# Moving the stationary operands of 256-column matmuls by 29 elements in SBUF

## The chip, the cores and the metric

The kernel runs on one core of one Trainium2 chip. The metric is device time in microseconds for one execution, as the median of several runs. A profile is one execution recorded by the hardware profiler; its span runs from the first to the last instruction and is a little shorter than the time of that execution.

## The reference, cut to what matters

The kernel computes two layers of a small encoder for 512 tokens of 1024 features, in float32. Each layer is a token mixer followed by a SwiGLU feed-forward, and each of the four parts has a norm with scale and shift ahead of it and a norm with a gate behind it.

```
def swiglu(h, w_gate, w_up, w_down):
    return (jax.nn.silu(h @ w_gate) * (h @ w_up)) @ w_down

for i in range(DEPTH):
    h = rms_norm(x, mix_pre_g[i]) * (1.0 + scale) + shift
    y = stick_breaking_mixer(...) if i % 2 == 0 else token_mixing_mixer(...)
    x = x + gate * rms_norm(y, mix_post_g[i])
    h = rms_norm(x, ffn_pre_g[i]) * (1.0 + scale) + shift
    y = swiglu(h, w_gate[i], w_up[i], w_down[i])
    x = x + gate * rms_norm(y, ffn_post_g[i])
```

The token mixer of layer 1 computes u and v as gelu(h @ w_in), mixes v over positions, and multiplies the two. The feed-forward is 2816 wide: gate and up are products of 512 x 1024 with 1024 x 2816 each, so they hold much of the arithmetic.

## The kernel before

Every float32 matrix product is made of three matmuls in the reduced fp32r format. An operand is split into a high part (a copy rounded to fp32r, made by ScalarE) and a low part (the difference, made by VectorE). `mm3` then adds high by high, low by high and high by low into one PSUM bank. In the profile these matmuls have one line, L107, and they are told apart by tiles: `r<-Sh,wh` writes bank `r`, streams `Sh` and holds `wh` as its stationary operand. TensorE first loads a stationary operand of 128 x 128 (the engine name PEld in the profile) and then streams the other operand past it, 256 or 512 columns at a time.

Weights arrive by DMA in `raw` buffers (`wload`, `block_loads`), in the order of a list named `stream`. `wemit` takes the next raw buffer, asks `wtile` for a pair of buffers `wh` and `wl`, and lets ScalarE and VectorE fill them. A pair rotates through five buffers (later six) of 1088 elements per partition. Only 1024 are needed for a weight tile, so a tile may begin a little way into its buffer, and `wtile` has an argument `at` for that.

In the kernel before, the start depends on how the tile is used:

- Weights of 512-column matmuls (q and k, v, the output projection, both down projections where they are not made by blocks) begin at element 16 of their buffers.
- Weights of 256-column matmuls begin at element 0. These are the gate and up weights of the first three units of each feed-forward (key `wgu`, tile `gu` in PSUM), the weights of u (key `win_u`, tile `u`), and the blocks of all later gate and up units (tile `r`).

The later gate and up units are made by `seven`. It takes a gate tile and an up tile together, as a two-by-two block product, and makes it with seven block products instead of eight. `blocks` prepares the weights for one such unit: `x` holds two blocks as they came, `b21` holds one more in a buffer of its own with 512 elements, and `t13` and `t24` hold sums of blocks. All of them are split into high and low parts. Each product runs over four slices of 128, three matmuls each, so a unit has 7 x 4 x 3 = 84 matmuls of 256 columns. There are 19 such units in each of the two feed-forwards. In all of these the weights are the stationary operand and the activations (`hTh`, `hTl`, `Sh`, `Sl`, in slots of 1024 elements) stream. Within a buffer the stationary slices are 128 elements, 512 bytes, apart, so a shift of the tile moves all its slices alike.

`down_blocks` prepares part of the weights of layer 1's down projection in the same kind of buffers, from element 0; those weights stream and are not part of the change. From the second seven-product unit on, the order of the instructions on TensorE, VectorE and ScalarE is written out as a chain (`pe["chain"]`, `dve.chain`, `act.chain`). `blocks` is a generator, and `seven` runs a piece of it behind each product, so that the preparation of the next unit lies beside the matmuls of this one.

One other place matters for reading the trace. The attention transposes 128-column slices of the `left` tiles, as stationary operands, against an identity (tile `tw`). These slices begin wherever the layout puts them, for example at elements 256, 257, 384, 385, 769, 771, 897 and 899 in one run of eight, because the scores of a head and key block are packed with one element between them. The transposes at layer boundaries (tile `tp`) take slices at multiples of 128.

In the program as it is built, the slots of the streaming `hT` and `S` tiles begin 64 bytes past a multiple of 128 bytes, and the buffers for `wh`, `wl` and `b21` begin at multiples of 128 bytes.

## Time and profile before

| what | value |
|---|---|
| median of 3 runs | 1123.85 us (1116.57 to 1124.16) |
| the profiled execution, its own time | 1124.99 us |
| its span | 1123.2 us |
| mean granted TensorE clock | 0.998 |
| DMA, whole span | 176.38 MB, 157 GB/s |
| instructions | 18514 |

The busy line gives for each engine its busy time, its share of the span and its count of instructions. PE is the matmul part of TensorE and PEld its weight loads, which overlap with matmuls. The chain of work that ended last is followed back from the last instruction and gives the share of the span by engine and by line. A table by stretches gives busy time and, in brackets, the records that touch the stretch, and behind them the granted clock, the busy share of the DMA engines and GB/s. The rows of groups give line, engine, operation, tiles, shape and count, then busy time and the mean length of one, then the idle time before them. Matmul lengths are modelled and overlap, so the distance between the starts of neighbours is what tells the pace. The rows in order of time have stamps in steps of 0.01 us, and neighbours of one kind are merged with a count.

### The profile page before, as it was taken

Reading aid. Unit: us, or ns where it says so; the run is one execution under the profiler, and the core shown is the slowest. Engines: PE = TensorE matmul, PEld = TensorE weight load, DVE = VectorE, ACT = ScalarE, POOL = GpSimd, SP = SyncE. Lnnn points to the kernel's source line nnn. Section 1 sums busy time; section 2 is a strip of 40 time slices with the busy share of each in tenths; the row PEclk is TensorE's granted clock in tenths of the full one; section 3 lists DMA queues with packets and bytes.
Section 4 is the critical chain, followed back from the end, with each engine's and each line's share of the span. In section 5 each row is a group of like instructions: output and inputs, shape, how many; then the busy total and the mean of one; then the engine's idle time right before and its main releaser. Section 6 shows DMA issues by size and latency. Waiting matters only on the chain.

```text
span 1123.2 us, 18514 instructions
## 1 busy us (share of the span) xinstructions
PE 1101.3 (98%) x7404; PEld 995.4 (89%) x7404; DVE 946.0 (84%) x1248; ACT 592.7 (53%) x982; POOL 29.5 (3%) x53
## 2 busy tenths in 40 slices
PE   6999999999999999999999999999999999999997
PEld 4787887788999999998888889988999999999995
DVE  4988999868979999879776867769979999899996
ACT  6445665656555555554253527437445555565652
POOL 0120100000000000000000000001000000000000
PEclk9999999999999999999999999999999999999999
DMA  8876435124424343359756375334224442333243
GB/s 322 340 233 208 148 101 159 61 65 153 164 76 169 132 147 130 109 204 335 266 194 249 132 261 164 105 123 153 97 95 151 145 148 91 105 113 94 76 139 125
DMA packets 51355, 176.38 MB, mean 157 GB/s; under 512 B 6074, under 2 KB 9146, under 8 KB 51268
## 3 DMA queue, kind: packets, MB, share of 16 engines
q1 hardware_dynamic: 48708, 166.81, 43.4%
q0 software_dynamic: 2560, 8.39, 2.1%
q8 instruction: 58, 0.95, 0.3%
q14 instruction: 29, 0.24, 0.1%
HBM read 164.69 MB, written 8.39 MB: 154 GB/s over the span
## 4 chain that ended last, share of the span: by engine, by line
PE 79%; DVE 10%; DMA 4%; ACT 4%; issue 2%; SPq 0%; DVEq 0%; ACTq 0%
PE r L107 32%; PE y L107 17%; PE pqk L107 7%; PE v L107 5%; PE gu L107 4%; PE u L107 4%; PE av L107 2%; PE z L107 2%; PE tw L115 1%; DMA raw<-in_wdn 1%; DVE wl L69 1%; DVE al L69 1%; DVE wl L176 1%; PE tp L115 1%; ACT wh L85 1%
## 5 line engine op out<-in xcount | busy, mean ns | idle before, releaser
L85 ACT ACTIVATE wh<-raw 128x1024 fp32r<-128x1024 f32 (+1 forms) x112 | 115.6, 1037 | 138.7 <-PE y L107 38.6
L107 PE MATMUL r<-Sh,wh 128*128 128x256 f32 x608 | 170.0, 280 | 0.0
L107 PE MATMUL r<-Sh,wl 128*128 128x256 f32 x608 | 169.9, 279 | 0.0
L107 PE MATMUL r<-Sl,wh 128*128 128x256 f32 x608 | 169.6, 279 | 0.0
L107 PE MATMUL y<-wh,as 128*128 128x512 f32 x480 | 149.9, 390 | 0.0
L176 DVE TENSOR_TENSOR wl<-raw,wh 128x1024 fp32r<-128x1024 f32 x87 | 105.9, 1221 | 51.0 <-ACT wh L85 50.5
L107 PEld LDWEIGHTS r<-Sh,wl 128*128 128x128 f32 x608 | 114.2, 188 | 0.0
L107 PEld LDWEIGHTS r<-Sl,wh 128*128 128x128 f32 x608 | 114.0, 188 | 0.1
L107 PEld LDWEIGHTS r<-Sh,wh 128*128 128x128 f32 x608 | 113.9, 187 | 0.1
L107 PEld LDWEIGHTS y<-wh,as 128*128 128x128 f32 x480 | 90.0, 188 | 18.6
L69 DVE TENSOR_TENSOR wl<-f,wh 128x1024 fp32r<-128x1024 f32 x87 | 103.2, 1218 | 1.6 <-ACT wh L85 1.6
L85 ACT ACTIVATE wh<-f 128x1024 fp32r<-128x1024 f32 x87 | 91.7, 1054 | 19.6 <-DVE f L69 11.9
L85 ACT ACTIVATE e<-r 128x256 f32<-128x256 f32 x114 | 43.8, 384 | 110.3 <-PE r L107 107.6
L107 PE MATMUL y<-wl,as 128*128 128x512 f32 x240 | 93.7, 390 | 0.0
L107 PE MATMUL r<-hTh,wh 128*128 128x256 f32 x304 | 85.2, 280 | 0.1
L107 PE MATMUL r<-hTh,wl 128*128 128x256 f32 x304 | 85.0, 279 | 0.0
L107 PE MATMUL r<-hTl,wh 128*128 128x256 f32 x304 | 84.8, 279 | 0.0
L107 PE MATMUL r<-hTh,b 128*128 128x256 f32 x304 | 59.8, 280 | 0.0
L85 ACT ACTIVATE wh<-rawx 128x1024 fp32r<-128x1024 f32 x38 | 40.3, 1060 | 33.8 <-PE r L107 30.5
L107 PEld LDWEIGHTS r<-hTh,wh 128*128 128x128 f32 x304 | 57.0, 187 | 0.8 <-DVE gu L69 0.8
L107 PEld LDWEIGHTS r<-hTh,wl 128*128 128x128 f32 x304 | 57.1, 188 | 0.0
L107 PEld LDWEIGHTS r<-hTl,wh 128*128 128x128 f32 x304 | 57.0, 188 | 0.0
(260 smaller groups left out, 2937.0 us busy)
## 6 DMA issues: line engine op xcount, KB each, us to landing
rawada<-in_ada SPq DMA_DIRECT2D x80, 512.0 KB, 5.6
rawy<-in_wy SPq DMA_DIRECT2D x38, 512.0 KB, 4.4
rawx<-in_wx SPq DMA_DIRECT2D x38, 512.0 KB, 3.8
raw<-in_wdown SPq DMA_DIRECT2D x22, 512.0 KB, 5.5
raw<-in_wdn SPq DMA_DIRECT2D x22, 512.0 KB, 3.8
raw<-in_wqk SPq DMA_DIRECT2D x16, 512.0 KB, 4.2
ada<-in_ada0p SPq DMA_DIRECT2D x12, 512.0 KB, 7.9
raw<-in_wgu SPq DMA_DIRECT2D x12, 512.0 KB, 3.6
```

Of the source, the lines that this page charges most:

```text
L69: b = getattr(nc.vector, op)(*args, **kw)
L85: b = nc.scalar.activation(*args, **kw)
L107: b = nc.tensor.matmul(o, l, r, start=start, stop=stop, skip_group_check=True)
L115: last_tp[0] = nc.tensor.transpose(o, i, ident)
L176: last_low[0] = nc.vector.tensor_tensor(l[:], raw[:], h[:].bitcast(F32), ALU.subtract)
```

## The change

A constant `SHORT = 29` is added. Weight tiles with the keys `wgu` and `win_u`, and the tiles `x`, `t13` and `t24` of `blocks`, begin at element 29 of their buffers. The two `b21` buffers grow from 512 to 544 elements and their 512 elements begin at 29 too. Everything else stays: the same instructions, the same order, the same transfers. 29 elements are 116 bytes.

```
+SHORT = 29
...
-        h, l = wtile(a, b, 0 if key[0] in ("wgu", "win_u") else 16)
+        h, l = wtile(a, b, SHORT if key[0] in ("wgu", "win_u") else 16)
...
-        x = wtile(KD, P)
+        x = wtile(KD, P, SHORT)
...
-        b21 = [fp.tile([P, 4, P], F32R, tag=f"b21{i}", name=nm("b21")) for i in range(2)]
+        b21 = [
+            fp.tile([P, 544], F32R, tag=f"b21{i}", name=nm("b21"))[
+                :, SHORT : SHORT + 512
+            ].rearrange("p (a b) -> p a b", a=4)
+            for i in range(2)
+        ]
...
-        t13 = wtile(KD, P)
+        t13 = wtile(KD, P, SHORT)
...
-        t24 = wtile(KD, P)
+        t24 = wtile(KD, P, SHORT)
```

## The prediction

> **What bounds the kernel now.** I read the page's busy line first, then the chain that ended last, then the busy time by stage, and last the groups of 256-column matmuls with the distance from one to the next.

> ```profile
> PE 1101.3 (98%) x7404; PEld 995.4 (89%) x7404; DVE 946.0 (84%) x1248; ACT 592.7 (53%) x982; POOL 29.5 (3%) x53
> ...
> PE 79%; DVE 10%; DMA 4%; ACT 4%; issue 2%; SPq 0%; DVEq 0%; ACTq 0%
> PE r L107 32%; PE y L107 17%; PE pqk L107 7%; PE v L107 5%; PE gu L107 4%; PE u L107 4%; PE av L107 2%; PE z L107 2%; PE tw L115 1%; DMA raw<-in_wdn 1%; DVE wl L69 1%; DVE al L69 1%; DVE wl L176 1%; PE tp L115 1%; ACT wh L85 1%
> ```

> TensorE bounds it: 79% of the chain. The three tiles whose weights are moved, r, gu and u, hold 32 + 4 + 4 = 40% of the span, so each per cent of their matmul time is worth 0.4%.

> ```profile
> core 0: us, PE busy (x) PEld busy (x) DVE busy (x) ACT busy (x) POOL busy (x), PEclk, DMA share, GB/s
> 277.40:313.60 36.20, 35.88 (x305) 35.66 (x304) 35.30 (x49) 22.25 (x38) 1.68 (x3) 1.00 0.49 165
> 313.60:503.50 189.90, 189.90 (x1606) 189.38 (x1605) 164.96 (x219) 101.38 (x172) 1.24 (x2) 1.00 0.39 135
> 639.50:725.10 85.60, 85.55 (x585) 79.25 (x584) 58.96 (x76) 39.70 (x55) 0.52 (x1) 1.00 0.51 166
> 773.80:810.90 37.10, 35.95 (x305) 35.71 (x305) 35.24 (x50) 20.81 (x37) 1.49 (x2) 1.00 0.44 143
> 810.90:1001.30 190.40, 190.34 (x1607) 189.60 (x1606) 165.83 (x218) 103.73 (x174) 0.00 (x0) 1.00 0.36 122
> ```

> The stages are, in this order: gate/up of layer 0 at the boundary (gu), its seven-product blocks (r), the token mixer's u with parts of v and sv, and gu and r of layer 1. In both r stages PE and its weight loads have no gap, the clock is granted in full and DMA stands at 0.36 to 0.39: only the time from one matmul to the next counts. In the gu stages VectorE is busy 35.30 of 36.20 us, so there PE is not alone on the path.

> ```profile
> line engine op names shapes xcount | busy us, mean ns | idle before us <-releasers
> L107 PE MATMUL r<-Sh,wh 128*128 128x256 f32 x608 | 170.0, 280 | 0.0
> L107 PE MATMUL r<-hTh,wh 128*128 128x256 f32 x304 | 85.2, 280 | 0.1
> L107 PE MATMUL r<-hTh,b 128*128 128x256 f32 x304 | 59.8, 280 | 0.0
> L107 PE MATMUL gu<-hTh,wh 128*128 128x256 f32 x192 | 54.0, 281 | 0.0
> L107 PE MATMUL r<-hTl,b 128*128 128x256 f32 x152 | 42.4, 279 | 0.0
> L107 PE MATMUL u<-hTh,wh 128*128 128x256 f32 x128 | 35.8, 280 | 0.0
> ```

> Each of the Sh, hTh, gu and u rows stands for three of one count (high by high, low by high, high by low), so the matmuls whose stationary operand moves are r: 3 x 608 + 3 x 304 + 304 + 152 = 3192, gu: 576, u: 384, together 4152. The 280 ns are a modelled length with overlap; what counts is the distance of starts:

> ```profile
> 820.00:940.00 120.00, 120.00 (x1022) 120.00 (x1021) 108.68 (x142) 64.08 (x109) 0.00 (x0) 1.00 0.39 137
> ```

> ```profile
> start us, us, engine line op out<-in xcount [idle before <-releaser]
> 1086.95 0.39 PE L107 MATMUL Y<-wh,ah 128*128 128x512 f32 x1
> ...
> 1088.31 0.28 PE L107 MATMUL Z<-wh,ah 128*128 128x256 f32 x1
> ...
> 1089.72 0.28 PE L107 MATMUL Z<-wh,Sh 128*128 128x256 f32 x1
> ```

> In r, 1022 records of 0.28 us overlap a stretch of 120 us: (120 + 0.28) / 1022 = 117.7 ns each. The other two distances are from the last stage: six 512-column matmuls in 1088.31 - 1086.95 = 1.36 us, 226.7 each, and twelve of 256 columns in 1.41 us, 117.5 each. So 256 more columns cost 109 ns, and a 256-column matmul pays 117.7 - 109 = 8.7 ns beside its columns. Those 8.7 ns, times 4152, are all that a better place could win; a worse place can cost as much or more.

> ```profile
> start us, us, engine line op out<-in xcount [idle before <-releaser]
> 283.07 1.03 PE L115 MATMUL tp<-identt,t 128*128 128x128 f32 x8
> ...
> 153.61 1.04 PE L115 MATMUL tw<-identt,left 128*128 128x128 f32 x8
> ```

> These are eight transposes each, with a new 128-column load for each one; the last is 0.27 long, so one takes (1.03 - 0.27) / 7 = 108.6 ns and (1.04 - 0.27) / 7 = 110 ns. Such a stream of short matmuls is paced by its loads, so I take about 109 ns as a load's own time, nearly the same as the 256 columns. A 256-column matmul thus has load and stream within 9 ns of each other, and anything that lengthens a load by more shows in full; a 512-column one hides it.

> **The change part by part.** *The new start of the stationary operand.* Weights of 4152 matmuls begin 29 elements, 116 bytes, later. No instruction, semaphore or transfer is added, removed or reordered; the two DMAs of a block land in raw buffers that stay. The only cost is in how the operand is read. The trace has no load of fp32r weights at such an offset under a 256-column stream, so I bound it. Lower end: the 8.7 ns vanish. Upper end, from the spread that load records show by operand:

> ```profile
> L107 PEld LDWEIGHTS W<-wh,Sl 128*128 128x128 f32 x44 | 8.4, 192 | 0.0
> L107 PEld LDWEIGHTS W<-wl,Sh 128*128 128x128 f32 x44 | 8.3, 188 | 0.0
> ```

> that is 192 - 188 = 4 ns. Nearest rows: weights in a slot with the stream from a weight buffer (Z and W, 117.5), weights in their buffer (r, 117.7) and in the b21 buffer (280 as the others) all agree, which speaks for a small effect. They are all placed at whole 512-byte steps from a buffer's start, however, so none is a test of 29. I take a gain of 1.5 ns: the middle of -8.7 and +4 is -2.3, drawn toward the rows that show 0. In r and u that is (3192 + 384) x 1.5 = 5.4 us. For gu I count nothing: its 576 x 1.5 = 0.9 us fall where VectorE is busy 97% and is what PE waits for; if VectorE were not there they would come on top. Ends: -8.7 x 3576 = -31 us, +4 x 4152 = +17 us.

> *The conversions that fill the shifted buffers* (ScalarE writes wh, VectorE reads wh and writes wl). The same two operations occur with buffers at 16 elements (the first two rows, layer 0's down projection) and at 0 (the third row, from the gu stage, and the last, from the blocks):

> ```profile
> L176 DVE TENSOR_TENSOR wl<-raw,wh 128x1024 fp32r<-128x1024 f32 x15 | 18.3, 1223 | 14.6 <-ACT wh L85 14.6
> ...
> L85 ACT ACTIVATE wh<-raw 128x1024 fp32r<-128x1024 f32 x15 | 15.8, 1060 | 47.4 <-PE y L107 30.3 <-DMA raw<-in_wdown 17.0
> ```

> ```profile
> L176 DVE TENSOR_TENSOR wl<-raw,wh 128x1024 fp32r<-128x1024 f32 x5 | 6.0, 1221 | 0.2 <-ACT wh L85 0.2
> ```

> ```profile
> L85 ACT ACTIVATE wh<-rawx 128x1024 fp32r<-128x1024 f32 x38 | 40.3, 1060 | 33.8 <-PE r L107 30.5
> ```

> They differ by 2 ns at most, so I cost them at nothing. What hides them in r is VectorE's slack, 120 - 108.68 = 11.3 us in 120, and ScalarE's 56 us. *The wider b21 buffers* (512 to 544 elements, four of them) move what lies behind them by whole 128-byte steps: no operation, nothing.

> Sum: 5.4 us off the profiled execution's 1124.99 gives 1119.6; that execution is 1.1 us above the median of 1123.85, so on the median's scale 1118.

> **The rivals.** *A larger gain.* If the place frees most of the 8.7 ns, say 4 to 8.7, r and u win 14 to 31 us: 1093 to 1110. For it: the 8.7 ns are there in every one of 4152 steps. VectorE would allow it, since in r it would become the bound only at 117.7 x 108.68 / 120 = 106.6 ns. Against it: three placements give one figure.

> [...]

> *Nothing happens.* The place of an operand doesn't matter to the stream at all: 1124. For it speaks that r, W and Z agree. [...]

> *VectorE becomes the bound.* If reads and writes at odd places are slower there, its slack of 11.3 us in 120 must go first. Its operations on shifted buffers in that stretch are these:

> ```profile
> L69 DVE TENSOR_TENSOR wl<-f,wh 128x1024 fp32r<-128x1024 f32 x24 | 28.2, 1218 | 0.0
> ...
> L69 DVE TENSOR_TENSOR wl<-rawx,wh 128x1024 fp32r<-128x1024 f32 x12 | 14.6, 1215 | 0.0
> ...
> L69 DVE TENSOR_TENSOR b<-rawy,b 128x512 fp32r<-128x512 f32 x12 | 8.2, 684 | 0.0
> ```

> Together 51 us, so they must take 22% longer before r feels it. If they took 40% longer, VectorE would need 108.68 + 20.4 = 129.1 us for what PE does in 120, and both r stages (380 us) would grow by 7.6%, 29 us: 1153. The rows at 16 elements speak against it.

> **How the numbers follow.** Small gain (up to 2.7 ns a step): 0.31, 1118. Larger gain: 0.29. No effect: 0.10, 1124. A loss of up to 1%: 0.06. The extra piece: 0.19, 1138. VectorE: 0.05, 1153. One per cent, about what a measurement of this kernel can tell from no change, is 11 us. Faster by more: 0.29; within: 0.31 + 0.10 + 0.06 = 0.47; slower by more: 0.19 + 0.05 = 0.24. The range for 8 in 10 goes from 1101 (6 ns won in r and u, 21 us, beyond which I leave about a third of the larger gain) to 1139, which takes in the extra piece. The likeliest case alone: 1113 to 1123.

> **What would show it.** Right: a stretch of 120 us inside r holds about 1035 matmul records instead of 1022 (116.2 ns each), both r stages are some 2.4 us shorter each, u half a us, and gu about as long as before. The operation times of L176 stay at 1220 to 1225. [...] The prediction is wrong if the stages of y, v or the last down projection, whose places don't change, move by as much as r does.

## The result, and the profile after

The changed kernel takes 1110.63 us (median of 6 runs, 1109.21 to 1114.39), beside 1123.9 us for the kernel before in the same comparison (6 runs, 1116.57 to 1125.94). The ratio is 0.9881, with a 95% interval of 0.9858 to 0.9903: 1.2% faster, where 1118 was forecast. The profiled execution is the slowest of the six, 1114.39 us with a span of 1112.6. Ratios here and below leave out slow executions (among the experiments one of 2202.20 us at start 16, one of 1336.16 us with the high part of b21 moved by 128 bytes, and one of 1129.42 us with the low parts moved); medians count them.

The busy line and the chain of the changed kernel's page (line numbers are two higher than before, so L109 is `mm3`'s matmul):

```profile
PE 1090.5 (98%) x7404; PEld 982.9 (88%) x7404; DVE 945.9 (85%) x1248; ACT 593.1 (53%) x982; POOL 29.5 (3%) x53
...
PE 82%; DVE 9%; ACT 4%; DMA 3%; issue 2%; SPq 0%; DVEq 0%; ACTq 0%
PE r L109 31%; PE y L109 17%; PE v L109 8%; PE pqk L109 7%; PE u L109 4%; PE gu L109 4%; PE av L109 2%; PE z L109 2%; PE tw L117 1%; DMA raw<-in_wdn 1%; DVE wl L71 1%; DVE al L71 1%; PE tp L117 1%; DVE wl L178 1%; PE ab L109 1%
```

PE lost 10.8 us of busy time and PEld 12.5, with the same 7404 matmuls; VectorE kept its 946 us. The table by stretches shows where. The first five rows are the five stages that the prediction quoted, cut at the same instructions; then the stretch of 120 us inside r; then two stretches of 30 us on either side of 327.6 us; and one inside u:

```profile
280.21:316.93 36.72, 36.20 (x306) 36.00 (x304) 35.60 (x49) 22.13 (x38) 1.67 (x3) 1.00 0.49 168
316.93:500.35 183.42, 183.42 (x1605) 182.84 (x1604) 164.63 (x219) 101.53 (x172) 1.12 (x2) 1.00 0.41 138
636.44:722.04 85.60, 85.52 (x585) 79.20 (x584) 58.90 (x76) 39.66 (x55) 0.52 (x1) 1.00 0.50 166
770.82:807.03 36.21, 35.04 (x305) 34.84 (x304) 34.93 (x50) 21.02 (x37) 1.49 (x2) 1.00 0.44 144
807.03:990.68 183.65, 183.43 (x1606) 182.49 (x1605) 165.78 (x219) 103.70 (x174) 0.00 (x0) 1.00 0.37 127
820.00:940.00 120.00, 120.00 (x1062) 120.00 (x1061) 113.20 (x147) 66.56 (x112) 0.00 (x0) 1.00 0.42 145
...
296.00:326.00 30.00, 30.00 (x252) 30.00 (x252) 24.34 (x37) 14.20 (x22) 0.00 (x0) 1.00 0.31 105
330.00:360.00 30.00, 30.00 (x267) 30.00 (x266) 27.33 (x37) 17.39 (x30) 0.00 (x0) 1.00 0.37 125
676.00:698.00 22.00, 22.00 (x185) 22.00 (x185) 16.50 (x19) 15.10 (x18) 0.00 (x0) 1.00 0.48 147
```

The two r stages went from 189.9 and 190.4 us to 183.42 and 183.65: 13.2 us, as much as the medians differ by (13.3). A stretch of u as long as before, 85.60 us, holds the same 585 records, so u gained nothing. Gate/up took 36.20 and 37.10 and takes 36.72 and 36.21. The profiled execution shows less than 13 us in all because it reaches gate/up 2.8 us later than the one of before (280.21 against 277.4), ahead of any moved operand. The stages between do not move.

The pace, worked out as in the prediction, is (length + 0.28) / records. Inside r it is 120.28 / 1062 = 113.3 ns, where it was 117.7. But in one and the same stage of one kernel there are two paces: 30.28 / 252 = 120.2 ns up to 326 us, and 30.28 / 267 = 113.4 from 330 on. In u it is 22.28 / 185 = 120.4. The starts of single matmuls repeat 113, 113, 114 in the one stretch and 120, 119, 121 (in the part in r 122, 120, 118) in the other, with the same instructions, operands at the same places, and the clock at 1.00. In the kernel before, the same two stretches have one pace, 30.28 / 257 = 117.8:

```profile
296.00:326.00 30.00, 30.00 (x257) 30.00 (x257) 24.91 (x37) 16.49 (x26) 0.00 (x0) 1.00 0.27 89
330.00:360.00 30.00, 30.00 (x257) 30.00 (x256) 26.35 (x36) 15.96 (x27) 0.00 (x0) 1.00 0.34 122
```

So the question was no longer only how much a place saves, but why one place has two paces, and what chooses. Below, a steady repeat of steps is called a pattern.

### The profile page after: what moved, and what is told of

The parts are those of the page before. It is cut to its first block, busy times and chain, and to the rows that moved or that the text cites. A ratio compares the mean times of both kernels' runs of the same rounds, so it can differ in the third digit from the quotient of the medians.

```text
span 1112.6 us, 18514 instructions
## 1 busy us (share of the span) xinstructions
PE 1090.5 (98%) x7404; PEld 982.9 (88%) x7404; DVE 945.9 (85%) x1248; ACT 593.1 (53%) x982; POOL 29.5 (3%) x53
## 4 chain that ended last, share of the span: by engine, by line
PE 82%; DVE 9%; ACT 4%; DMA 3%; issue 2%; SPq 0%; DVEq 0%; ACTq 0%
PE r L109 31%; PE y L109 17%; PE v L109 8%; PE pqk L109 7%; PE u L109 4%; PE gu L109 4%; PE av L109 2%; PE z L109 2%; PE tw L117 1%; DMA raw<-in_wdn 1%; DVE wl L71 1%; DVE al L71 1%; PE tp L117 1%; DVE wl L178 1%; PE ab L109 1%
## 5 line engine op out<-in xcount | busy, mean ns | idle before, releaser
L109 PE MATMUL r<-Sh,wh 128*128 128x256 f32 x608 | 168.1, 276 | 0.0
L109 PE MATMUL r<-Sh,wl 128*128 128x256 f32 x608 | 167.9, 276 | 0.0
L109 PE MATMUL r<-Sl,wh 128*128 128x256 f32 x608 | 167.9, 276 | 0.0
L109 PE MATMUL y<-wh,as 128*128 128x512 f32 x480 | 150.0, 390 | 0.0
L109 PEld LDWEIGHTS r<-Sh,wh 128*128 128x128 f32 x608 | 114.1, 188 | 0.3 <-ACT e L87 0.2
L109 PEld LDWEIGHTS r<-Sl,wh 128*128 128x128 f32 x608 | 114.2, 188 | 0.1
L109 PEld LDWEIGHTS r<-Sh,wl 128*128 128x128 f32 x608 | 114.1, 188 | 0.0
L109 PEld LDWEIGHTS y<-wh,as 128*128 128x128 f32 x480 | 90.0, 188 | 18.7
L71 DVE TENSOR_TENSOR wl<-f,wh 128x1024 fp32r<-128x1024 f32 x87 | 103.3, 1221 | 1.4 <-ACT wh L87 1.4
L109 PE MATMUL y<-wl,as 128*128 128x512 f32 x240 | 93.7, 390 | 0.0
L109 PE MATMUL r<-hTh,wh 128*128 128x256 f32 x304 | 84.2, 277 | 0.2 <-DVE gu L71 0.2
L109 PE MATMUL r<-hTh,wl 128*128 128x256 f32 x304 | 84.0, 276 | 0.0
L109 PE MATMUL r<-hTl,wh 128*128 128x256 f32 x304 | 84.0, 276 | 0.0
L109 PE MATMUL r<-hTh,b 128*128 128x256 f32 x304 | 58.0, 276 | 0.0
L109 PEld LDWEIGHTS r<-hTh,wh 128*128 128x128 f32 x304 | 57.1, 188 | 0.9 <-DVE gu L71 0.9
L109 PEld LDWEIGHTS r<-hTl,wh 128*128 128x128 f32 x304 | 57.1, 188 | 0.0
L109 PEld LDWEIGHTS r<-hTh,wl 128*128 128x128 f32 x304 | 57.1, 188 | 0.0
```

The lines of the kernel that those rows point to most:

```text
L71: b = getattr(nc.vector, op)(*args, **kw)
L109: b = nc.tensor.matmul(o, l, r, start=start, stop=stop, skip_group_check=True)
```

## The experiments

Letters of theories hold only within the quoted text in which they stand. "Step" is the distance from one 256-column matmul to the next. The step of r is taken from the stretch from 350 to 470 us of each profile; 1061 or 1062 records are 113.3 ns, 1021 or 1022 are 117.7.

**Other starts.** Four kernels differ from the changed one by the constant alone.

```
-SHORT = 29
+SHORT = 28        (and 1, 3, 16)
```

> Weights of gate/up and u begin at element 28 (112 bytes, a multiple of 16) instead of 29. Theory A, the place relative to the stream counts (weights now 52 bytes past the stream's place in a stretch of 128 bytes, 64 before): 28 is 4 bytes from 29, so the step in r is near 113.5 ns, the time near 1110 us. Theory B, the odd start inside a piece of 16 bytes counts: 28 is aligned like 0, the step is 117.7 ns, the time near 1124 us.

> Weights of gate/up and u begin at element 1 (4 bytes). Theory A (place relative to the stream): 4 bytes from the place of before, so the step in r stays near 117.7 ns, 1124 us. Theory B (odd start inside 16 bytes; 29 and 1 are both one element past a multiple of four): the step is that of 29, 113.5 ns, 1110 us.

> Weights of gate/up and u begin at element 16 (64 bytes), as those of the 512-column matmuls do, at the same place in 128 bytes as the stream. Theory A gives a step of its own, not 117.7; where before's r and u matmuls were followed by a load at that place, single steps took 115 to 117 ns, so 115.5 ns and about 1116 us. Theory B: aligned to 16 bytes, so 117.7 ns and 1124 us.

> Weights of gate/up and u begin at element 3 (12 bytes), the same distance to the other side of a 128-byte multiple as 29. Theory A, if only the size of the distance counts: as 29, 113.5 ns, 1110 us; if its sign counts: not faster, 117.7 ns or more, 1124 us or more. Theory B (any start off 16 bytes): 113.5 ns, 1110 us.

| start | time, us | ratio to before | records, 350 to 470 us | step of r, ns |
|---|---|---|---|---|
| 28 | 1126.58 | 1.0025 (1.0004 to 1.0047) | 1021 | 117.8 |
| 1 | 1126.45 | 1.0016 (1.0000 to 1.0032) | 1021 | 117.8 |
| 16 | 1135.39 | 1.0103 (1.0061 to 1.0145) | 1003 | 119.9 |
| 3 | 1114.80 | 0.9923 (0.9892 to 0.9953) | 1061 | 113.4 |

29 and 3 are fast, 28, 1 and 16 are not. Neither theory fits: 28 speaks against A, 1 against B, and 16, with 119.9 ns, came out slower than either had it. In the run at 3, gate/up ran at 18.28 / 149 = 122.7 ns between 300 and 318 us, and r changed to the fast step in the middle of a product at 325 us, as the changed kernel did at 327.6. So 3 was a worse place than 0 until something happened there.

**The matmuls by themselves, and r alone.** One kernel holds only runs of 48 such matmuls, at 32 starts, with nothing on the other engines; it computes nothing of the reference and was executed once. In the cut below `turns` makes eight transposes, `at` is the start of the weights and `mat` that of the stream. The other kernel shifts r (the blocks and b21) and leaves gu and u at 0.

```
+    for at in range(32):
+        turns()
+        stream("c" + letters(at), 16, 256, at)
...
+    for mat in range(32):
+        turns()
+        stream("i" + letters(mat), 16, 256, 0, mat)
```

```
-        h, l = wtile(a, b, SHORT if key[0] in ("wgu", "win_u") else 16)
+        h, l = wtile(a, b, 0 if key[0] in ("wgu", "win_u") else 16)
```

> A kernel of matmuls alone; it computes nothing of the reference. Loads of 128 x 128 fp32r weights under streams of 256 or 512 columns, 48 in a run, the stream 64 bytes past a multiple of 128 as in the kernel; the weights begin at each of the elements 0 to 31 in turn, and each run of 256 columns is entered once straight from 512-column matmuls (runs a..) and once from eight transposes (c..). One series keeps the weights at 0 and moves the stream (i..), one has 512 columns (e..), one puts one matmul of 16 to 192 columns ahead of a run at 29 (k..), two have stationary operands of 64 and 32 columns under 512 (g, h). Theory L (a run settles in one of a few steady patterns; the start of the weights decides which there are, the entry which is taken): 0, 16, 28 and 1 give 117.7, 120, 117.7 and 118 ns; 29 and 3 give 113.5 in some runs and 120 to 121.6 in others, 29 from 512 columns the slow one, and a short matmul ahead can turn it to 113.5; 512 columns give 226.7 or more. Theory M (other engines' traffic in SBUF decides): every start gives the same step in every run, as no other engine works here. [...]

> Only the blocks of the seven-product units begin at 29; the weights of the first units (wgu) and of u are back at 0. By the trace after, gu and u won nothing (means of 117.5 and 118 ns, half of their runs at 113.5 and half at 120), so this kernel should take the time of the full change, 1110 us, within 3 us. If gu and u carry part of the gain (0.4 ns times 960 is all that their means show), it is slower by no more than 1 us. If r's own pattern depends on entering from gu at 29, r in layer 0 could be at 113.5 from its start (3.5 us won, 1107) or fall to 120 throughout (1133).

The steps of the last twelve matmuls of a run lie between 113.3 and 123.3 ns: entered from 512-column matmuls they are 117.8 at 0, 118.3 at 1, 123.3 at 3, 120 at 16, 117.75 at 28 and 113.3 at 29. But a run at 29 entered from transposes has 120, and one at 3 has 120 too; it had been expected the other way round for 29. The strongest pair needs no other place at all. Runs `ca` and `iq` have the same weights and the same stream, byte for byte, and both follow eight transposes; by the order in which the six PSUM banks rotate, they write the same bank as well. The third and the last matmul of each, in order of time:

```profile
248.04 0.28 PE L62 MATMUL ca<-Sh,wl 128*128 128x256 f32 x1
...
253.34 0.28 PE L62 MATMUL ca<-Sh,wl 128*128 128x256 f32 x1
...
725.50 0.28 PE L62 MATMUL iq<-Sh,wl 128*128 128x256 f32 x1
...
730.60 0.28 PE L62 MATMUL iq<-Sh,wl 128*128 128x256 f32 x1
```

45 steps take 5.30 us in `ca`, 117.8 ns each, and 5.10 us in `iq`, 113.3 each. That a place has one step, and that other engines' accesses make the difference, are both out: VectorE and ScalarE stand still here. A run falls into one of several steady patterns, from 113.3 to 123.3 ns here, most within a few matmuls, and `ca` and `iq` keep theirs to the last of their 48. The patterns seen differ from start to start, but the start of the weights doesn't settle which is taken, and neither does the kind of matmul ahead, since `ca` and `iq` agree in both. What in the entry chooses was not found.

The kernel with r alone shifted takes 1111.04 us (ratio 0.9877, 0.9857 to 0.9898), no worse than the whole change: gu and u give nothing. Its profile holds a second pair like `ca` and `iq`, inside the kernel itself. Gate/up has its weights at 0 there, at the same addresses as before. From 295 to 313 us of layer 0, first in this kernel and then in the kernel before:

```profile
295.00:313.00 18.00, 18.00 (x162) 18.00 (x161) 17.57 (x26) 10.11 (x15) 0.00 (x0) 1.00 0.37 118
```

```profile
295.00:313.00 18.00, 18.00 (x155) 18.00 (x154) 17.58 (x26) 10.62 (x16) 0.00 (x0) 1.00 0.36 119
```

That is 18.28 / 162 = 112.8 ns beside 18.28 / 155 = 117.9; by single starts, 113.3 from 293.5 us on. So gate/up at 0 now and then enters the fast pattern by itself.

**A disturbance at the entry, and the other half of the change.** The first two add one matmul of 64 columns ahead of seven runs, whose result the next matmul overwrites, once with the weights at 29 and once at 0. The third shifts gu and u alone and leaves the blocks and b21 at 0.

```
+            if f == 0 and lo == 0:
+                mm(gp[:, :64], w[0][0][:, 0, :], hB(self.hT, 0, lo, 64)[0], True, False)
...
+            if f == NH:
+                mm(R1[:, :64], W["B11"](0)[0], S["A11"](0)[0][:, :64], True, False)
...
+        if m < 2:
+            mm(ub[:, :64], w[0][:, 0, :], hB(hT, 0, lo, 64)[0], True, False)
```

> The change, and one extra 64-column matmul (its result is overwritten by the first matmul of the unit) ahead of seven runs: the first gate/up unit of each layer, the first seven-product unit of each layer, both parts of the first u unit and the second u unit. In the trace after, 585 steps of gu, u and of r's start sit at 120 ns, and in the kernel of matmuls alone a short matmul put all eight runs at 29 to 113.3. Theory L (the entry decides): these 585 steps fall by 6.4 ns, 3.7 us, the extra matmuls cost about 0.11 us each, 0.8 us, so about 3 us less than the change, 1107 to 1108 us. Rival (the slow steps of gu and u come from the other engines at the boundary, VectorE 97% busy there): they stay at 120, and the time is 1111 us.

> The same seven extra matmuls, but the weights at 0 as before. In the kernel of matmuls alone the same run at 0 stepped at 117.7 once and at 113.3 another time, so 0 has the fast pattern too. Theory L: at least some of the seven runs enter at 113.3, and r, if it does, keeps it until disturbed; between 1111 us (all of r) and 1124 us (none of it). Rival (29 is needed): every run stays at 117.7 ns and the time is that of before plus 0.8 us, 1125 us.

> Only the weights of the first gate/up units and of u begin at 29; the blocks of the seven-product units, b21 too, are back at 0. If r's gain belongs to 29, r steps at 117.7 and the time is that of before, 1124 us, within 1 us. If r keeps the pattern with which it is entered, and gu hands over the fast one in layer 1 (as it does in the trace after, from 786 us on), r of layer 1 runs at 113.3 even at 0: 1596 times 4.4, 7 us less, 1117 us.

At 29 the time is 1108.94 us (0.9874, 0.9844 to 0.9903), and the long stretch of u goes to 113.3 ns but for a few steps at its beginning, while gate/up behind the transposes of layer 0 stays at 120. At 0 it is 1112.53 (0.9898, 0.9865 to 0.9930), and with gu and u alone 1110.65 (0.9891, 0.9853 to 0.9930). In the last two, r has its weights at 0, just as in the kernel before, and yet steps at 113.3 ns for most of its length. So the gain of r doesn't need r's weights at 29. With gu and u alone the time is below both values forecast: in layer 1 r keeps the 113.3 ns with which it comes from gate/up, and in layer 0 it comes at 113.3, drops to 117.7 at a longer step of 0.14 us at 316.1 us, and returns to 113.3 at a product that reads b21. The other run at 0 has r change at such products in both layers, and both kernels still had the b21 buffers of 544 elements.

**The wider b21 buffers.** The next three are the changed kernel with every start back at 0; the kernel before with the seven short matmuls, and so with b21 buffers of 512; and the changed kernel with the short matmul ahead of every gate/up unit.

```
-SHORT = 29
+SHORT = 0
```

> The changed kernel with SHORT at 0: every weight begins where it did before, and only the two b21 buffers stay 544 elements wide, which moves what lies behind them by whole 128-byte steps. Two runs with all or some weights at 0 (with a short matmul ahead of seven runs, and with only gu and u at 29) came to 1110.65 and 1112.53 us, with r at 113.3 ns after a product that streams past b21; both had this wider b21 too. Theory A (several steady patterns, the entry and disturbances choose): with no kick and no shifted weight the entry is that of before, so r stays near 117.7 ns and the time within 3 us of before, about 1124, unless a b21 product flips it as it did there. Theory B (the new address of b21 and what lies behind it gives the gain): r flips at the b21 product near 325 us to 113.3 ns and the time is 1110 to 1114. Theory C (the offset of 29 is needed somewhere): 1124, r at 117.7 throughout.

> The kernel before, b21 with 512 elements and all 256-column weights at 0, with one more matmul of 64 columns ahead of seven runs (gate/up of each layer, the first block product of each layer, and the u units of the first half), whose result the next matmul overwrites: 7 x 0.11 = 0.8 us more work. Theory A (the entry chooses the pattern): r in at least one layer goes to 113.3 ns, 1596 x 4.4 = 7 us each, so 1111 to 1118. Theory B (the wider b21 does it): r stays at 117.7 ns in both layers, 1124 to 1126.

> The changed kernel (29) with the short matmul ahead of every gate/up unit, of the first block product of each layer and of two u units. With the seven kicks alone the gate/up units of layer 0 that follow the transposes ran at 120 ns from 286 to 316 us, some 250 steps. If the entry chooses the pattern, these go to 113.3 ns too: 250 x 6.7 = 1.7 us less on PE, of which VectorE lets through part, and five more kicks cost 0.55 us: 1107 to 1109 beside 1108.9. If the pattern after transposes is not chosen by the entry, they stay at 120 ns: 1109.5.

With nothing but the wider buffers the time is 1114.91 us (0.9900, 0.9885 to 0.9916). In its table by stretches the step goes from 16.28 / 138 = 118.0 to 16.28 / 144 = 113.1 ns; the change comes at 342.2 us:

```profile
325.00:341.00 16.00, 16.00 (x138) 16.00 (x137) 14.08 (x18) 8.49 (x14) 0.00 (x0) 1.00 0.45 158
344.00:360.00 16.00, 16.00 (x144) 16.00 (x143) 14.73 (x20) 9.20 (x16) 0.00 (x0) 1.00 0.38 136
```

The kernel before with the short matmuls stays at 1126.93 (1.0018, 0.9996 to 1.0041). So the disturbance at the entry did nothing at 0, and what turned r in the earlier run with it was the wider buffers. At 29 the disturbance works on the step: with one ahead of every gate/up unit the time is 1108.90 us (0.9850, 0.9836 to 0.9863), not clearly apart from the changed kernel's 0.9881 (0.9858 to 0.9903). In u and in gate/up of layer 0 its step is 18.28 / 161 = 113.5 ns:

```profile
674.00:692.00 18.00, 18.00 (x161) 18.00 (x160) 14.00 (x18) 13.55 (x16) 0.00 (x0) 1.00 0.42 131
295.00:313.00 18.00, 18.00 (x161) 18.00 (x160) 17.60 (x26) 10.36 (x16) 0.00 (x0) 1.00 0.35 116
```

The same stretches of the changed kernel have 153 and 152 records, 120 ns:

```profile
678.00:696.00 18.00, 18.00 (x153) 18.00 (x152) 15.13 (x18) 14.02 (x16) 0.00 (x0) 1.00 0.48 146
296.00:314.00 18.00, 18.00 (x152) 18.00 (x152) 17.27 (x25) 8.85 (x14) 0.00 (x0) 1.00 0.34 116
```

**What about the buffers does it.** In the program as built, all the 256-column weights that the change moves begin, in the kernel before, at multiples of 256 bytes. Buffers of 544 elements lie 2176 bytes apart, so every second one of b21 begins at an odd multiple of 128. In the four kernels with weights at 0 or 3 and a change of step at a b21 product, it was each time the product with that buffer (there are two buffers in turn and 19 units a layer, so these are the second, fourth and so on of layer 0 and the first, third and so on of layer 1). Two kernels have the same spacing and differ by the start alone; a third has all moved weights at 32 elements, 128 bytes.

```
-        b21 = [fp.tile([P, 4, P], F32R, tag=f"b21{i}", name=nm("b21")) for i in range(2)]
+        b21 = [
+            fp.tile([P, 576], F32R, tag="b210", name=nm("b21"))[
+                :, 0:512                      (the other kernel: 32:544)
+            ].rearrange("p (a b) -> p a b", a=4),
+            fp.tile([P, 4, P], F32R, tag="b211", name=nm("b21")),
+        ]
```

> The kernel before, with the buffers of the high part of b21 576 elements wide, in place of 512, and the block at their start; the low part stays at 512. High parts begin at 210176 and 212480 and low parts at 214784 and 216832, all multiples of 256 bytes, but high and low no longer lie a multiple of 2048 apart. Theory S (the spacing gives the change of pattern): r goes to 113.3 ns in both layers after a few products, 1112 to 1116. Theory H (an odd multiple of 128 gives it): r stays at 117.7 ns, 1123 to 1126.

> As the run at 0, with the same buffers, but the high part of b21 begins 32 elements, 128 bytes, into its buffer: 210304 and 212608, both odd multiples of 128. Everything else begins at multiples of 256. Theory H: r changes to 113.3 ns at a b21 product of each layer, as early as or earlier than with one such buffer of two (342 and 824 us there), and the time is 1110 to 1115. Theory S: the same time as the run at 0, whichever that is.

> The changed kernel with SHORT at 32 in place of 29: all weights of gu, u and r begin 128 bytes into their buffers, at odd multiples of 128 (of the b21 buffers, 544 wide, every second one is back at a multiple of 256). Theory H in its strong form (at an odd multiple of 128 a run always settles at 113.3 ns): r, gu and u all at 113.3, 1106 to 1110. In its weak form (there both patterns exist, and a change of place between 0 and 128 is what brings a run from the one to the other): r changes at some b21 product to 113.3, gu and u stay at 117.7, 1111 to 1116. If neither holds, r stays at 117.7, about 1125, as at 28 and 1.

High part of b21 at a multiple of 256: 1124.53 us (0.9994, 0.9972 to 1.0016). The same buffers, 128 bytes further: 1112.12 (0.9887, 0.9856 to 0.9917). The row from 350 to 470 us of the first, and then that of the second:

```profile
350.00:470.00 120.00, 120.00 (x1021) 120.00 (x1021) 109.32 (x142) 65.09 (x111) 0.00 (x0) 1.00 0.39 139
```

```profile
350.00:470.00 120.00, 120.00 (x1062) 120.00 (x1061) 112.81 (x148) 67.90 (x116) 0.00 (x0) 1.00 0.39 137
```

In the second kernel the step changes at the very first b21 product of layer 0. In order of time, `b` marks the product:

```profile
315.26 0.28 PE L107 MATMUL r<-hTl,wh 128*128 128x256 f32 x1
315.38 0.28 PE L107 MATMUL r<-hTh,wl 128*128 128x256 f32 x1
315.50 0.28 PE L107 MATMUL r<-hTh,b 128*128 128x256 f32 x1
315.61 0.28 PE L107 MATMUL r<-hTl,b 128*128 128x256 f32 x1
...
315.96 0.28 PE L107 MATMUL r<-hTl,b 128*128 128x256 f32 x1
...
316.30 0.28 PE L107 MATMUL r<-hTl,b 128*128 128x256 f32 x1
```

Ahead of it a matmul starts each 120 or 110 ns by the stamps (117.7 on the mean), and from 315.96 to 316.30 three take 340, 113.3 each. Spacing is out: of these two kernels, only the one with loads from another place modulo 256 bytes is fast. Such a load is a chance and not a switch. With every start at 0 and the wider buffers, and with the seven short matmuls added to that, r stood at 117.7 ns ahead of nine products of the buffer at an odd multiple of 128, and four of them turned it to 113.3; of seven products of the other buffer none did. In the kernel before, with and without the short matmuls, and in the first kernel here none of 114 did. In the second kernel all three products that found r at 117.7 turned it. But its layer 1 was not won at a b21 product, as had been expected: r came at 113.3 from gate/up, which has its weights at 0 and had settled so by itself:

```profile
784.00:802.00 18.00, 18.00 (x161) 18.00 (x160) 17.90 (x28) 10.63 (x16) 0.00 (x0) 1.00 0.30 94
```

With all moved weights at 32 the time is 1108.67 us (0.9865, 0.9831 to 0.9899): r is at 113.3, but gate/up enters at 117.7 in both layers and settles at 113.3 only from 291 and 780 us on, and the long stretch of u stays at 117.7. An odd multiple of 128 is thus no faster place. It has the two patterns that 0 has.

**The 29 without the side effect, and the change of place without b21.** In the first, high and low part of b21 share one buffer of 1088 elements, so that all moved weights begin 116 bytes past a multiple of 256. In the second, the kernel before gets only its low parts moved by 32 elements; its b21 is as it was.

```
+        both = fp.tile([P, 1088], F32R, tag="b21", name=nm("b21"))
+        b21 = [
+            both[:, SHORT + o : SHORT + o + 512].rearrange("p (a b) -> p a b", a=4)
+            for o in (0, 512)
+        ]
```

```
-            for n in ("wh", "wl")
+            for n, o in (("wh", at), ("wl", at or 32))
```

> The changed kernel at 29, with the high and low part of b21 side by side in one buffer of 1088 elements, so that every b21 slice too begins 116 bytes past a multiple of 256, as all the other moved weights do. Theory H (r leaves the slow pattern only when a load comes from another place modulo 256 bytes): r keeps the pattern with which its layer is entered. If layer 0 enters at 120 ns, as the changed kernel did until 327 us, it stays there: 1400 steps x 6.7 = 9 us more than the changed kernel's 1110.6 for each layer that does, 1117 to 1132. If both layers happen to enter at 113.3 ns, 1109 to 1112. Theory 29 (the place of 29 by itself settles at 113.3 in the end, the b21 product being just a long enough time): r turns to 113.3 in both layers within some 40 us, 1109 to 1113.

> The kernel before, b21 as it was (all four buffers at multiples of 256 bytes), all high parts of weights at 0, and the low parts of the weights that begin at 0 placed 32 elements, 128 bytes, into their buffers (gu, u, the blocks, and the blocks of the last projection). In each group of three matmuls the load then goes from 0 to 0 to 128. Theory H in the form that a load from the other half of 256 bytes frees the stream: gu, u and r run at 113.3 ns nearly throughout, 1106 to 1110. If only a rare change does it and frequent ones hinder, or if it is a matter of the b21 product alone: some other step, 1112 to 1135. Nothing happens: 1124.

The first takes 1109.50 us (0.9880, 0.9845 to 0.9915). In its profiled execution the fast step begins inside gate/up already, at 284.5 us, with all loads at like places, and it lasts through r in both layers:

```profile
283.37 0.28 PE L109 MATMUL gu<-hTl,wh 128*128 128x256 f32 x1
...
284.44 0.28 PE L109 MATMUL gu<-hTl,wh 128*128 128x256 f32 x1
284.55 0.28 PE L109 MATMUL gu<-hTh,wl 128*128 128x256 f32 x1
...
285.12 0.28 PE L109 MATMUL gu<-hTl,wh 128*128 128x256 f32 x1
```

Nine steps in 1.07 us are 118.9 ns, and five in 0.57 us are 114. In u, entered from 512-column matmuls, it stays at 120 as in the changed kernel. So r can be fast by another way: it is entered from a run that has already settled at 113.3. My theory that only a change of place frees r falls, therefore. How much of that is owed to 29 is less sure, since gate/up at 0 settled at 113.3 as well in two profiles above, and these b21 buffers were not tried with the starts at 0. What speaks for 29 is the count: five of the six runs took 1107.08 to 1111.94 us, where the 11 runs of the kernel before beside them took 1119.65 to 1127.30. The sixth took 1120.92; a layer of r that stays at 120 would do that, but no profile shows it. So the wider buffers suffice, by a direct comparison, and the 29 likely suffices too; the change contains both.

The second takes 1115.77 us (0.9904, 0.9869 to 0.9940), with the runs that the ratio counts from 1107.27 to 1117.71. In its profile, of a run of 1107.89, gate/up, r and u all have the fast step for most of their length; in u it is 18.28 / 161 = 113.5:

```profile
674.00:692.00 18.00, 18.00 (x161) 18.00 (x161) 14.94 (x18) 13.47 (x16) 0.00 (x0) 1.00 0.48 147
...
284.00:289.00 5.00, 5.00 (x44) 5.00 (x43) 4.87 (x7) 4.43 (x7) 1.50 (x2) 1.00 0.72 233
```

A change of place in every third load thus goes with the fast step without any help of b21, in u too, whose long stretch no other profile with u's weights at 0 shows at 113.3. But not every run has it: in the same profile one of gate/up stays at (5 + 0.28) / 44 = 120 ns from 284 to 289 us. Whether a frequent change knocks a run out as well as in is not shown, and none of its longer executions was profiled.

## Why the prediction was wrong, point by point

**The bound was right.** TensorE's pace in r was the whole matter: the two r stages gave 13.2 us, and the medians differ by 13.3.

**The size of the step failed.** 13.3 us came off where 5.9 were forecast. The term was "(3192 + 384) x 1.5 = 5.4 us", for the steps of r and u, with 1.5 ns drawn toward zero because three placements (r, W and Z, b21) showed one figure, 117.7. r gained 117.7 - 113.3 = 4.4 ns, which in 3192 steps would be 14.0 us. Before 327.6 us layer 0 paid back 0.6 (some 90 steps at 120 in place of 113.3). u gained nothing, since over half of its steps were at 120 (218 of 375) and only a third at 113.3 (121), 117.8 on the mean. What was wrong is the notion behind the number: that a place has a step. The three rows that agreed were three runs in one pattern, not three measurements of a free choice. The other pattern is within reach at the very same addresses, as `ca` and `iq` and gate/up at 0 show. The rival "a larger gain" had the right size per step for r, 4.4 ns in its 4 to 8.7; but its mechanism, a place that frees the stream, is not what the runs show either, so that its number fits by luck. The direction was luck in part as well: starts 1, 28 and 16 leave the old place too, and none of them gained.

**The wider b21 buffers, costed at nothing, failed.** "No operation, nothing" is right as far as work goes; but by itself this part gives 1114.91 us, 9.7 less than the 1124.64 measured beside it. It was the one part of the change that altered where neighbouring loads stand to each other, and I looked at it only for what it adds.

**gu was right for a reason that only half holds.** It gave 0.5 us back in layer 0 and took 0.9 off in layer 1. VectorE is indeed busy 35.60 of 36.72 us in layer 0. But there the step did not gain either: it was 120 over most of the stage. Where the step is fast VectorE does take some of it back, in the waits for its `t` ahead of the transposes: in the run with a short matmul ahead of every gate/up unit, the second eight transposes begin 1.22 us after the start of the last matmul ahead of them, where in the kernel before it was 0.60.

```profile
289.45 0.28 PE L109 MATMUL gu<-hTh,wl 128*128 128x256 f32 x1
290.67 0.33 PE L117 MATMUL tp<-identt,t 128*128 128x128 f32 x1 [0.94 <-DVE t L71]
```

```profile
290.19 0.28 PE L107 MATMUL gu<-hTh,wl 128*128 128x256 f32 x1
290.79 0.33 PE L115 MATMUL tp<-identt,t 128*128 128x128 f32 x1 [0.33 <-DVE t L69]
```

**The conversions were right.** In the stretch from 820 to 940 us of the changed kernel VectorE's passes over shifted buffers take 1218 and 1220 ns, where the prediction's rows had 1215 and 1218:

```profile
L71 DVE TENSOR_TENSOR wl<-f,wh 128x1024 fp32r<-128x1024 f32 x26 | 30.6, 1220 | 0.0
...
L71 DVE TENSOR_TENSOR wl<-rawx,wh 128x1024 fp32r<-128x1024 f32 x12 | 14.6, 1218 | 0.0
```

The matmul row of r, over the whole kernel, has a mean length of 276 ns where it had 280: this modelled length moved by a little less than the step.

```profile
L109 PE MATMUL r<-Sh,wh 128*128 128x256 f32 x608 | 168.1, 276 | 0.0
```

**The rivals.** The extra piece per load is out: no run shows such a term. The 1138 us stand for 3.4 ns more in each of 4152 steps, and r at 29 and at 3 stepped at 113.3 and 113.4 ns, less than the 117.7 of before. "Nothing happens" is out as well: in the kernel of matmuls alone the start of the weights alone moved the settled step, from 117.8 ns at 0 to 120 at 16 with 256 columns and from 226.6 at 12 to 236.7 at 5 with 512. That 512 columns hide what lengthens a load was an estimate: by the prediction a load takes 109 ns (the distance of transposes with a new load each, 108.6 to 110), about half of 226.6, and yet the start of the weights counted there too. In what way it bears on the stream is not shown. VectorE is no bound yet: it is busy 113.20 of 120 us in r, which would bind at 113.3 x 0.943 = 106.9 ns. y, v and the last projection stood still, as said.

## What to carry to other kernels

Measure the distance between starts of like matmuls in several stretches before pricing it, and look whether one stretch differs from another: several steady paces at the same addresses, as 117.8 and 113.3 ns in `ca` and `iq`, mean that a row is the pattern the run happened to fall into, not a property of the place. Split a change of addresses into its parts, the buffers that merely shift included, and run each alone, because where two parts can each suffice, neither is missed when it alone is taken away. Where a run can settle in several ways, a neighbouring load from another place can be worth 1%, as here (1112.12 us beside 1124.53), but a fix is only as good as the spread of its runs (1108.39 to 1108.96 with short matmuls ahead of every gate/up unit at 29, 1107.27 to 1117.71 for the moved low parts).
